# Weight pools laid at whole pages from the stationary tiles, and the down products split in halves around the up group, in a one-core fp32 encoder block

## The chip, the cores and the metric

The kernel runs on one core of one Trainium2 chip. The metric is the device time of one execution in microseconds (us). The kernel before took 1651.87 us, the median of three runs (1650.79, 1651.87 and 1653.72). Its engines are called by their names in the profile: PE is the matrix engine, PEld its loads of stationary tiles, DVE the vector engine, ACT the scalar engine, POOL the GpSimd engine, SP the queue that issues the DMAs.

## The reference

One layer on an input of 256 rows by 2048 columns, all in float32, with a last RMSNorm behind it:

```python
xn = rms_norm(h, norm1_g)
z_a, q, c_kv, q_idx, k_idx, w_idx, gates = split(xn @ w_in)
y_a = spatial_gating_unit(gelu(z_a), ...)          # u * (W_s layer_norm(v) + b)
y_b = indexer_sparse_attention(q, rms_norm(c_kv), q_idx, k_idx, w_idx, w_uk, w_uv)
g_a, g_b = split(sigmoid(gates))
h = h + (g_a * (y_a @ w_oa) + g_b * (y_b @ w_ob)) @ w_out
hn = rms_norm(h, norm2_g)
h = h + (silu(hn @ w_ff_gate) * (hn @ w_ff_up)) @ w_ff_down     # 2048 -> 5632 -> 2048
return rms_norm(h, final_g)
```

## The kernel before

**Three products for one.** Every large product is split into high and low parts. `split` (lines 70 to 78) makes `h` on ACT (line 74) and `l`, the rest, on DVE (line 75). `mm3` (lines 88 to 91) issues three matmuls for each pair of tiles: high by high, high by low, low by high. A matmul keeps a stationary tile of 128 x 128 and streams a moving tile of up to 512 columns past it; while it streams, PE loads the stationary tile of the next one (PEld).

**The first part: everything up to the second norm.** The weights come in chunks of 128 x 1024 through `wchunk` (lines 80 to 86): a DMA into `raw`, ACT makes `wh`, DVE makes `wl`, all three in the pool `wp` with four buffers each. Two helpers consume them. `nat_group` (lines 93 to 106) has the activations stationary and 512 columns of `wh` or `wl` moving; it does the groups named `v`, `u`, `g` (gates), `oa`, `ob`, `out` and `vv`. A group over 16 steps of 128 rows is 16 x 2 x 3 = 96 matmuls; `vv` has 4 steps and 24. There are 4 groups each of `v`, `u`, `oa`, `ob`, `out` and `vv`, and 8 of `g`. `tr_group` (lines 108 to 126) has it the other way round, the weights stationary and 256 columns of the activations moving: 2 groups `qi` and 4 groups `q` of 192 matmuls, and 4 groups `k` of 48.

**Where the tiles lie.** Pools take their places in a partition in the order in which they are opened (lines 48 to 56): `const`, `tp` (20 tiles of 4096 bytes: all activations in high and low parts), then `np` (11 tiles of 4096), `sp` (small tiles of many sizes, 17,376 bytes together), `tq` (4 tiles of 4096) and `wp` (12 tiles of 4096). The build's addresses are 18,336 for `tp`, 100,256 for `np`, 145,312 for `sp`, 162,688 for `tq` and 179,072 for `wp`. A page here means 4096 bytes. `sp` is four pages and 992 bytes long, so `tq` and `wp` begin 992 bytes past a whole number of pages from `tp`. From each other `tq` and `wp` are whole pages. The attention output `yb` of its first two groups is kept in `tq`, that of the last two in `tp`; so the first 48 matmuls of an `ob` group have stationary tiles whole pages from the moving ones, and the last 48 do not.

**The second part: the feed-forward.** `pre.close()` (line 497) gives back `np`, `sp`, `tq` and `wp`, and the pools `wq` and `fp` take their room directly behind `tp` and whole pages from it. `wq` has three buffers for `raw` tiles of 128 x 2048, three each for `wh` and `wl` of that size, two each of 128 x 1536, and one for `sums`. The gate and up products go through `s_group` (lines 520 to 572), a Strassen form that needs seven products for eight. It takes eight weight quads in the order `(0, 4, 1, 5, 2, 3, 6, 7)`. For a quad below 4, DVE first makes four sums of the raw weights (lines 534 to 536), then both the raw quad (1536 columns) and the sums (2048) are split, and PE runs 21 matmuls, of which the first nine need the raw quad alone (from the second such quad on). For the others only the raw quad is split, and PE runs 24. A group is 4 x 21 + 4 x 24 = 180 matmuls of 512 columns. `plain_group` (lines 574 to 585) is the plain form.

The loop at the end runs over five pairs of blocks, counted from 0. One turn is: the gate group `fg` of pair i, with the 16 transposes `a_pt` of the block before (through `beside`, line 558) ahead of its last 12 matmuls; the down products `fd` of pair i-1, which are four groups n of 8 x 2 x 3 = 48 matmuls; the up group `fu` of pair i. PE's order is the order of the program; DVE, ACT and SP get theirs from the scheduler, each a fixed list that is worked off in order. After an up group DVE has to combine its sums (lines 569 and 571) and to multiply by the gate (line 608); after each down group it adds the result to `hn[n]` (line 617).

Of the kernel before, what the change touches and what calls it, by code (L numbers as in the profile page):

```python
# [13 lines left out]
ALU = mybir.AluOpType  # L14
AX = mybir.AxisListType

P = 128
# [23 lines left out]
def block_kernel(ctx: ExitStack, tc: tile.TileContext, a, out):  # L41
# [5 lines left out]
    nc = tc.nc  # L47
# [3 lines left out]
    aux_p = ctx.enter_context(tc.tile_pool(name="aux", bufs=4, space=bass.MemoryType.PSUM))  # L51
    pre = ExitStack()
    np_ = pre.enter_context(tc.tile_pool(name="np", bufs=11))
    sp = pre.enter_context(tc.tile_pool(name="sp", bufs=1))
    tq = pre.enter_context(tc.tile_pool(name="tq", bufs=4))
    wp = pre.enter_context(tc.tile_pool(name="wp", bufs=4))

    def t_tile(name, dt=F32R):
        return tp.tile([P, 4, T], dt, tag="T", name=name)
# [10 lines left out]
    def split(h, l, src, scale=None):  # L70

        hf = h.bitcast(F32)
        if scale is None:
            nc.scalar.activation(h, src, AF.Copy)  # L74
            nc.vector.tensor_tensor(l, src, hf, op=ALU.subtract)  # L75
        else:
            nc.scalar.activation(h, src, AF.Copy, scale=scale)
            nc.vector.scalar_tensor_tensor(l, src, scale, hf, op0=ALU.mult, op1=ALU.subtract)
# [9 lines left out]
    def mm3(o, lh, ll, rh, rl, start, stop, **kw):  # L88
        nc.tensor.matmul(o, lh, rh, start=start, stop=False, **kw)  # L89
        nc.tensor.matmul(o, lh, rl, start=False, stop=False, **kw)  # L90
        nc.tensor.matmul(o, ll, rh, start=False, stop=stop, **kw)  # L91

    def nat_group(w, ks, x, name):


        acc = [acc_tile(f"{name}_{t}") for t in range(2)]
        for c in range(len(ks) // 2):
            wh, wl = wchunk(w[c], 1024)
            for j in range(2):
                i = 2 * c + j  # L100
                xh, xl = x(ks[i])
                for t in range(2):
                    s = slice(t * P, (t + 1) * P)
                    mm3(acc[t], xh[:, s], xl[:, s], wh[:, j * 512:(j + 1) * 512],
                        wl[:, j * 512:(j + 1) * 512], i == 0, i == len(ks) - 1)
        return acc
# [109 lines left out]
    def row_rstd(ss, name):  # L216
        s2 = sp.tile([P, 2], F32, name=f"{name}_s2")
        nc.vector.tensor_reduce(s2, ss.rearrange("p n t -> p t n"), axis=AX.X, op=ALU.add)
        r = const.tile([P, 2], F32, name=f"{name}_r")
        rsqrt(r, s2, 1.0 / D, EPS, 2, name)  # L220
        return r
# [92 lines left out]
    for t in (1, 0):  # L314
        w = (t + 1) * P
        nc.vector.memset(score[t][0:CHUNK, w - CHUNK:w], NEG)
        for i in range(TOPK // 8):
# [4 lines left out]
                                op0=ALU.is_gt, op1=ALU.mult)  # L322
# [104 lines left out]
    for n in range(4):  # L427
        for j in range(2):
# [5 lines left out]
                                           op0=ALU.add, op1=ALU.mult)  # L434
# [4 lines left out]
    def of(pairs):  # L439
        def f(k):  # L440
            h, l = pairs[k // 4]
            return h[:, k % 4], l[:, k % 4]
        return f
# [10 lines left out]
    for n in range(4):  # L454
        ga = gate(n)
        acc = nat_group(a["w_oa"][n], KS, of(ya), f"oa{n}")
# [3 lines left out]
    for n in range(4):  # L460
        gb = gate(4 + n)
        acc = nat_group(a["w_ob"][n], KS, of(yb), f"ob{n}")
# [9 lines left out]
    hn, hT = [], []  # L472
    for n in range(4):
        hx = tp.tile([P, 2, 512], F32, tag="T", name=f"h{n}")
        nc.sync.dma_start(hx, x_nat[n])
        acc = nat_group(a["w_out"][n], KS, of(mx_t), f"out{n}")
# [6 lines left out]
        else:  # L483
            for b in range(2):
                k = 4 * n + 2 * b
# [8 lines left out]
    r2 = row_rstd(ss2, "r2")  # L494
# [6 lines left out]
    def f_tile(name):  # L501
        return fp.tile([P, 2, 512], F32, tag="F", name=name, bufs=3)

    def quad(src):
        raw = wq.tile([P, 4, 512], F32, tag="raw", name="raw")
        nc.sync.dma_start(raw, src)
        return raw

    def quad_split(raw, n=4):
        h, l = (wq.tile([P, n, 512], F32R, tag=f"w{z}{n}", name=f"w{z}", bufs=n - 1 if n < 4 else 3) for z in "hl")  # L510
        split(h, l, raw)
        return h, l
# [61 lines left out]
    def plain_group(chunks, x, n_k, name, bank=acc_tile):  # L574

        acc = [bank(f"{name}_{t}") for t in range(2)]
        for i, c in enumerate(chunks):
            wh, wl = quad_split(quad(c))
            for j in range(4):
                k = 4 * i + j  # L580
                for t in range(2):
                    xh, xl = x(k, t)
                    mm3(acc[t], xh, xl, wh[:, j], wl[:, j], k == 0, k == n_k - 1)
        return acc

    at = {}

    def a_operand(b, s):
        h, l = t_tile(f"ah{b}"), t_tile(f"al{b}")
        transposed(s, f"a{b}", h, l)  # L590
        at[b] = (h, l)

    def gate_blocks(i, beside):
        f, _ = s_group(a["w_fg"][i], f"fg{i}", beside)
        s = [f_tile(f"s{i}_{j}") for j in range(2)]
        for j in range(2):
            for t in range(2):
                f(t, j, s[j][:, t])
                nc.scalar.activation(s[j][:, t], s[j][:, t], AF.Silu, scale=r2[:, t:t + 1])
        return s  # L600

    def up_blocks(i, s):
        f, u = s_group(a["w_fu"][i], f"fu{i}")
        for j in range(2):
            for t in range(2):
                f(t, j)
        for j in range(2):
            nc.vector.tensor_tensor(s[j], s[j], u[:, 2 * j:2 * j + 2], op=ALU.mult)

    def down(b0, n_b):  # L610

        for n in range(4):
            acc = plain_group([a["w_fd"][n, b0 + j] for j in range(n_b)],
                              lambda k, t: tuple(z[:, k % 4, t * P:(t + 1) * P] for z in at[b0 + k // 4]),
                              4 * n_b, f"fd{n}", aux_tile if n < 2 else acc_tile)
            for t in range(2):
                nc.vector.scalar_tensor_tensor(hn[n][:, t], acc[t], r2[:, t:t + 1], hn[n][:, t],
                                               op0=ALU.mult, op1=ALU.add)
            yield n

    def plain_x(k, t):
        if k < 2 * NS:
# [6 lines left out]
    b = NFB - 1  # L629
    for i in range(b // 2 + 1):  # L630
        done = s

        def transposes():
            if done is not None:
                for j in range(2):
                    a_operand(2 * i - 2 + j, done[j])
        if i < b // 2:
            s = gate_blocks(i, transposes)
            if i:
                for _ in down(2 * i - 2, 2):  # L640
                    pass
            up_blocks(i, s)

    acc = plain_group([a["w_fg10"][c] for c in range(4)], plain_x, KT, f"fg{b}", aux_tile)
    transposes()
# [3 lines left out]
    acc = plain_group([a["w_fu10"][c] for c in range(4)], plain_x, KT, f"fu{b}")  # L649
    for t in range(2):  # L650
        nc.vector.tensor_tensor(s[:, t], acc[t], s[:, t], op=ALU.mult)
    kept = []
    for n in down(b - 2, 2):
        if n < 2:
            raw = quad(a["w_fd"][n, b])
            kept.append([])
            for c in range(2):
                h, l = (tp.tile([P, 2, 512], F32R, tag="T", name=z) for z in ("kept_h", "kept_l"))
                split(h, l, raw[:, 2 * c:2 * c + 2])
                kept[n] += [(h[:, k], l[:, k]) for k in range(2)]  # L660
        if n == 1:
            a_operand(b, s)
# [6 lines left out]
    for i in range(2):  # L669
        f = f_tile(f"fg{i}")  # L670
# [106 lines left out]
```

## Time and profile before

| what | us |
|---|---|
| median of three runs | 1651.87 |
| the profiled execution | 1649.41 |
| its span | 1647.6 |
| PE busy | 1608.0 |
| DVE busy | 1098.7 |
| ACT busy | 778.8 |

In the profile a matmul's record is longer than the time to the next one's start, since matmuls are pipelined; the pace of PE is read from the starts. A timeline gives the start of each instruction, its length, the engine, the line, the operation, the tile written and the tiles read, the shapes, and in square brackets the idle time of the engine ahead of it with what ended it. The first feed-forward matmul starts at 898.23 us.

### The profile page before, as it was taken

To read this page: it belongs to the slowest core of one execution; us is meant where nothing else is said; L and a number is where in the kernel's file an instruction comes from. 1 tells how busy PE (TensorE), PEld (TensorE's weight loads), DVE (VectorE), ACT (ScalarE), POOL (GpSimd) and SP (SyncE) were. 2 spreads that over 40 slices of the span, in tenths; PEclk is the share of its full clock that TensorE was granted. 3 is DMA by queue.
4 is the path that set the end of the run, shared out by engine and by line. 5 is a ranking of instruction groups with operands and counts; after the bars stand their busy time and mean duration, and the time that the engine had idled before them with its cause. 6 is when DMAs were issued, how large, how long until landed. Compare 5 with 4: busy or idle time off the path is not lost.

```text
span 1647.6 us, 19647 instructions
## 1 busy us (share of the span) xinstructions
PE 1608.0 (98%) x7834; PEld 1337.3 (81%) x7834; DVE 1098.7 (67%) x1208; ACT 778.8 (47%) x815; POOL 1.6 (0%) x8
## 2 busy tenths in 40 slices
PE   9999999999999999999997998999999999999997
PEld 8988989989788888888885777887887788788886
DVE  5795665565744444555565888788788778777565
ACT  6654454554544444444354464454454544454442
POOL 0000000000000000000000000000000000000000
PEclk9999999999999999999998999999999999999999
DMA  8645545545455555555664544554564554555561
GB/s 304 224 138 191 186 163 182 180 163 192 137 180 191 187 185 190 188 183 183 200 205 157 188 181 176 205 200 163 200 222 161 204 204 179 182 201 198 210 230 51
DMA packets 69115, 307.48 MB, mean 187 GB/s; under 512 B 8160, under 2 KB 8416, under 8 KB 52128
## 3 DMA queue, kind: packets, MB, share of 16 engines
q1 hardware_dynamic: 69024, 306.24, 53.4%
q8 instruction: 61, 1.00, 0.2%
q14 instruction: 30, 0.25, 0.0%
HBM read 304.11 MB, written 2.10 MB: 186 GB/s over the span
## 4 chain that ended last, share of the span: by engine, by line
PE 77%; DVE 12%; ACT 4%; issue 4%; DMA 2%; ACTq 0%; SPq 0%; DVEq 0%
DVE wl L75 7%; ACT wh L74 4%; PE fd L91 4%; PE fd L90 4%; PE fd L89 4%; PE g L89 4%; PE g L90 4%; PE g L91 4%; PE u L91 2%; PE q L123 2%; PE oa L90 2%; PE oa L89 2%; PE v L90 2%; PE v L89 2%; PE u L89 2%
## 5 line engine op out<-in xcount | busy, mean ns | idle before, releaser
L75 DVE TENSOR_TENSOR wl<-raw,wh 128x1024 fp32r<-128x1024 f32 (+3 forms) x434 | 640.3, 1477 | 406.9 <-ACT wh L74 406.6
L74 ACT ACTIVATE wh<-raw 128x1024 fp32r<-128x1024 f32 (+3 forms) x434 | 545.2, 1262 | 578.8 <-PE g L91 90.0
L74 ACT ACTIVATE wh<-sums 128x2048 fp32r<-128x2048 f32 x40 | 76.7, 1917 | 173.8 <-DVE sums L536 152.6
L75 DVE TENSOR_TENSOR wl<-sums,wh 128x2048 fp32r<-128x2048 f32 x40 | 91.7, 2292 | 64.3 <-ACT wh L74 64.3
L89 PE MATMUL fd<-wh,ah 128*128 128x512 f32 x320 | 124.6, 389 | 0.0
L91 PE MATMUL fd<-wh,al 128*128 128x512 f32 x320 | 124.5, 389 | 0.0
L90 PE MATMUL fd<-wl,ah 128*128 128x512 f32 x320 | 124.5, 389 | 0.0
L91 PE MATMUL g<-wh,xl 128*128 128x512 f32 x256 | 102.5, 400 | 0.0
L89 PE MATMUL g<-wh,xh 128*128 128x512 f32 x256 | 102.3, 400 | 0.0
L90 PE MATMUL g<-wl,xh 128*128 128x512 f32 x256 | 101.5, 396 | 0.0
L121 PE MATMUL q<-xh,wh 128*128 128x256 f32 x256 | 71.5, 279 | 0.0
L123 PE MATMUL q<-xl,wh 128*128 128x256 f32 x256 | 71.5, 279 | 0.0
L124 PE MATMUL q<-xh,wl 128*128 128x256 f32 x256 | 71.5, 279 | 0.0
L90 PEld LDWEIGHTS fd<-wl,ah 128*128 128x128 f32 x320 | 60.1, 188 | 12.5
L89 PEld LDWEIGHTS fd<-wh,ah 128*128 128x128 f32 x320 | 60.1, 188 | 12.5
L91 PEld LDWEIGHTS fd<-wh,al 128*128 128x128 f32 x320 | 60.1, 188 | 12.4
L90 PE MATMUL fg_c<-wl,hh 128*128 128x512 f32 x160 | 62.6, 392 | 0.5 <-DVE wl L75 0.5
L89 PE MATMUL fg_c<-wh,hh 128*128 128x512 f32 x160 | 63.0, 393 | 0.0
L91 PE MATMUL fg_c<-wh,hl 128*128 128x512 f32 x160 | 62.4, 390 | 0.0
L89 PE MATMUL fu_c<-wh,hh 128*128 128x512 f32 x160 | 62.2, 389 | 0.0
L90 PE MATMUL fu_c<-wl,hh 128*128 128x512 f32 x160 | 62.2, 389 | 0.0
L91 PE MATMUL fu_c<-wh,hl 128*128 128x512 f32 x160 | 62.2, 389 | 0.0
(303 smaller groups left out, 3431.6 us busy)
## 6 DMA issues: line engine op xcount, KB each, us to landing
raw<-in_w_fg SPq DMA_DIRECT2D x44, 1024.0 KB, 4.8
raw<-in_w_fu SPq DMA_DIRECT2D x44, 1024.0 KB, 4.8
raw<-in_w_fd SPq DMA_DIRECT2D x44, 1024.0 KB, 4.8
raw<-in_w_z SPq DMA_DIRECT2D x64, 512.0 KB, 3.5
raw<-in_w_g SPq DMA_DIRECT2D x64, 512.0 KB, 3.3
raw<-in_w_q SPq DMA_DIRECT2D x32, 512.0 KB, 3.2
raw<-in_w_oa SPq DMA_DIRECT2D x32, 512.0 KB, 3.2
raw<-in_w_ob SPq DMA_DIRECT2D x32, 512.0 KB, 3.2
```

Of the source, the lines that this page charges most:

```text
L74: nc.scalar.activation(h, src, AF.Copy)
L75: nc.vector.tensor_tensor(l, src, hf, op=ALU.subtract)
L89: nc.tensor.matmul(o, lh, rh, start=start, stop=False, **kw)
L90: nc.tensor.matmul(o, lh, rl, start=False, stop=False, **kw)
L91: nc.tensor.matmul(o, ll, rh, start=False, stop=stop, **kw)
L121: nc.tensor.matmul(o, wh[:, s], xh, start=(i == 0 and ct % 2 == 0), stop=False, skip_group_check=True)
L123: nc.tensor.matmul(o, wh[:, s], xl, start=False, stop=False, skip_group_check=True)
L124: nc.tensor.matmul(o, wl[:, s], xh, start=False, stop=last, skip_group_check=True)
```

## The change

The pool `sp` is opened last, behind `wp`. In the build `tq` then begins at 145,312, `wp` at 161,696 and `sp` at 210,848: `wp` is now 35 pages from `tp`. The generator `down` over all four n becomes `down_one` for one n, the turn calls it for n = 0 and 1 behind the gate group and for n = 2 and 3 behind the up group, and the accumulators of the down products alternate between the two PSUM pools (before: n = 0 and 1 in one, 2 and 3 in the other).

```diff
     np_ = pre.enter_context(tc.tile_pool(name="np", bufs=11))
-    sp = pre.enter_context(tc.tile_pool(name="sp", bufs=1))
     tq = pre.enter_context(tc.tile_pool(name="tq", bufs=4))
     wp = pre.enter_context(tc.tile_pool(name="wp", bufs=4))
+    sp = pre.enter_context(tc.tile_pool(name="sp", bufs=1))
...
-    def down(b0, n_b):
-        for n in range(4):
-            acc = plain_group([a["w_fd"][n, b0 + j] for j in range(n_b)],
...
-                              4 * n_b, f"fd{n}", aux_tile if n < 2 else acc_tile)
...
-            yield n
+    def down_one(b, n):
+        acc = plain_group([a["w_fd"][n, b + j] for j in range(2)],
...
+                          8, f"fd{n}", acc_tile if n % 2 else aux_tile)
...
             s = gate_blocks(i, transposes)
-            if i:
-                for _ in down(2 * i - 2, 2):
-                    pass
+            for n in (0, 1) if i else ():
+                down_one(2 * i - 2, n)
             up_blocks(i, s)
+            for n in (2, 3) if i else ():
+                down_one(2 * i - 2, n)
...
-    for n in down(b - 2, 2):
+    for n in range(4):
+        down_one(b - 2, n)
```

On PE, at the end of up group 1, gate group 2 (`fg_m`) followed at once:

```order
L89 MATMUL fu_c_8714<-wh,hh_7517 128x512
L90 MATMUL fu_c_8714<-wl,hh_7517 128x512
L91 MATMUL fu_c_8714<-wh,hl_7518 128x512
L89 MATMUL fg_m_8987<-wh,hS_h 128x512
L90 MATMUL fg_m_8987<-wl,hS_h 128x512
L91 MATMUL fg_m_8987<-wh,hS_l 128x512
```

and in the changed kernel a down group does:

```order
L89 MATMUL fu_c_8586<-wh,hh_7517 128x512
L90 MATMUL fu_c_8586<-wl,hh_7517 128x512
L91 MATMUL fu_c_8586<-wh,hl_7518 128x512
L89 MATMUL fd_0_8859<-wh,ah_8397 128x512
L90 MATMUL fd_0_8859<-wl,ah_8397 128x512
L91 MATMUL fd_0_8859<-wh,al_8398 128x512
```

So 96 matmuls of the down products now stand between an up group and the next gate group, and 96 instead of 192 between a gate group and its up group (from turn 1 on; turn 0 has none).

On DVE, at the same place, the list before went from combining the up group (`fu_c`, then `s`, the product with the gate) straight to the sums of the second quad of the next gate group and their split:

```order
L571 TENSOR_TENSOR fu_u<-fu_c_8714,fu_u 128x512
L608 TENSOR_TENSOR s_0_8441<-s_0_8441,fu_u 128x1024
L608 TENSOR_TENSOR s_1_8442<-s_1_8442,fu_u 128x1024
L534 TENSOR_TENSOR sums<-raw 128x1024
L535 TENSOR_TENSOR sums<-sums,raw 128x512
L75 TENSOR_TENSOR wl<-raw,wh 128x1536
L536 TENSOR_TENSOR sums<-sums,raw 128x512
L75 TENSOR_TENSOR wl<-sums,wh 128x2048
```

In the changed kernel the same sums stand behind the additions of the last down group (`h`, `fd`), with the first quad's sums split, and two further `wl`, ahead of them:

```order
L535 TENSOR_TENSOR sums<-sums,raw 128x512
L536 TENSOR_TENSOR sums<-sums,raw 128x512
L75 TENSOR_TENSOR wl<-sums,wh 128x2048
L75 TENSOR_TENSOR wl<-raw,wh 128x1536
L75 TENSOR_TENSOR wl<-raw,wh 128x2048
L617 SCALAR_TENSOR_TENSOR h_7367<-fd_0_8923,r_r,h_7367 128x512
L617 SCALAR_TENSOR_TENSOR h_7367<-fd_1_8924,r_r,h_7367 128x512
L534 TENSOR_TENSOR sums<-raw 128x1024
L535 TENSOR_TENSOR sums<-sums,raw 128x512
L536 TENSOR_TENSOR sums<-sums,raw 128x512
L75 TENSOR_TENSOR wl<-sums,wh 128x2048
```

The combining of the up group has moved ahead, to the start of the second half of the down products. On SP the loads follow PE's order (the first place where they differ):

```order
 L506 DMA raw<-in_w_fg 128x2048 x8
-L506 DMA raw<-in_w_fd 128x2048 x8
+L506 DMA raw<-in_w_fd 128x2048 x4
 L506 DMA raw<-in_w_fu 128x2048 x8
+L506 DMA raw<-in_w_fd 128x2048 x4
 L506 DMA raw<-in_w_fg 128x2048 x8
```

The down products' eight loads are split into four ahead of the up group's and four behind them.

## Rows read from the trace of the kernel before

**Rows 1.** The page, its head: span, busy time and share, instructions of each engine.

```profile
span 1647.6 us, 19647 instructions
PE 1608.0 (98%) x7834; PEld 1337.3 (81%) x7834; DVE 1098.7 (67%) x1208; ACT 778.8 (47%) x815; POOL 1.6 (0%) x8
```

**Rows 2.** Windows: length, busy us by engine (count), granted clock, DMA share, GB/s.

```profile
429.70:893.00 463.30, 463.30 (x2025) 372.27 (x2023) 238.40 (x235) 199.58 (x222) 0.00 (x0) 1.00 0.55 186
1041.00:1174.00 133.00, 130.00 (x574) 106.80 (x573) 107.54 (x87) 62.63 (x42) 0.00 (x0) 0.99 0.53 192
```

**Rows 3.** Timeline of PE: first matmul of one oa group, and of the g group behind.

```profile
462.67 0.40 PE L89 MATMUL oa<-wh,yah 128*128 128x512 f32 x1
...
485.07 0.40 PE L89 MATMUL g<-wh,xh 128*128 128x512 f32 x1
```

**Rows 4.** Timeline of PE in one ob group: 44 intervals in each half.

```profile
642.56 0.39 PE L89 MATMUL ob<-wh,ybh 128*128 128x512 f32 x1
...
652.54 0.40 PE L91 MATMUL ob<-wh,ybl 128*128 128x512 f32 x1
...
653.47 0.40 PE L89 MATMUL ob<-wh,ybh 128*128 128x512 f32 x1
...
663.74 0.40 PE L91 MATMUL ob<-wh,ybl 128*128 128x512 f32 x1
```

**Rows 5.** Timeline of PE: first matmul of up group 1, and of gate group 2.

```profile
1089.04 0.39 PE L89 MATMUL fu_m<-wh,hS_h 128*128 128x512 f32 x1
...
1129.84 0.39 PE L89 MATMUL fg_m<-wh,hS_h 128*128 128x512 f32 x1
```

**Rows 6.** Timeline of PE, 256 columns: 192 intervals of q, 23 of last.

```profile
176.78 0.28 PE L121 MATMUL q<-xh,wh 128*128 128x256 f32 x1
...
199.19 0.28 PE L121 MATMUL k<-cT_h,wh 128*128 128x256 f32 x1
...
1624.82 0.28 PE L89 MATMUL last<-wh,ah 128*128 128x256 f32 x1
...
1627.57 0.28 PE L91 MATMUL last<-wh,al 128*128 128x256 f32 x1
```

**Rows 7.** Chain of work that ended last: start, us, what; the transposes of four turns.

```profile
1041.17 1.75 PE a_pt L152 x16
...
1173.62 1.75 PE a_pt L152 x16
...
1305.05 1.75 PE a_pt L152 x16
...
1438.22 1.75 PE a_pt L152 x16
```

**Rows 8.** Timeline of PE in gate group 2: its 55th and 56th matmul.

```profile
1142.59 0.51 PE L89 MATMUL fg_m<-wh,hS_h 128*128 128x512 f32 x1 [0.34 <-ACT wh L74]
1144.92 0.50 PE L90 MATMUL fg_m<-wl,hS_h 128*128 128x512 f32 x1 [1.82 <-DVE wl L75]
```

**Rows 9.** Timeline of DVE at the start of gate group 2.

```profile
1131.65 1.28 DVE L569 TENSOR_TENSOR fu_u<-fu_c,fu_u 128x512 f32<-128x512 f32 x2
...
1134.05 2.35 DVE L608 TENSOR_TENSOR s<-s,fu_u 128x1024 f32<-128x1024 f32 x2
1136.31 1.22 DVE L534 TENSOR_TENSOR sums<-raw 128x1024 f32<-128x1024 f32 x1
...
1138.18 1.75 DVE L75 TENSOR_TENSOR wl<-raw,wh 128x1536 fp32r<-128x1536 f32 x1
...
1142.57 2.29 DVE L75 TENSOR_TENSOR wl<-sums,wh 128x2048 fp32r<-128x2048 f32 x1 [2.04 <-ACT wh L74]
```

**Rows 10.** Timeline of ACT in the down groups that start at 1045.5 us.

```profile
1056.64 1.92 ACT L74 ACTIVATE wh<-raw 128x2048 fp32r<-128x2048 f32 x1 [3.52 <-PE fd L91]
```

**Rows 11.** Timeline of DVE where those down groups end and up group 1 starts.

```profile
1088.90 1.40 DVE L617 SCALAR_TENSOR_TENSOR h<-fd,r_r,h 128x512 f32<-128x512 f32 x2
1091.23 2.29 DVE L75 TENSOR_TENSOR wl<-sums,wh 128x2048 fp32r<-128x2048 f32 x1 [0.93 <-ACT wh L74]
```

More of the change, by code (lines that the diff above doesn't have):

```diff
@@ L608, in up_blocks @@
             nc.vector.tensor_tensor(s[j], s[j], u[:, 2 * j:2 * j + 2], op=ALU.mult)
-    def down(b0, n_b):
-        for n in range(4):
-            acc = plain_group([a["w_fd"][n, b0 + j] for j in range(n_b)],
-                              lambda k, t: tuple(z[:, k % 4, t * P:(t + 1) * P] for z in at[b0 + k // 4]),
-                              4 * n_b, f"fd{n}", aux_tile if n < 2 else acc_tile)
-            for t in range(2):
-                nc.vector.scalar_tensor_tensor(hn[n][:, t], acc[t], r2[:, t:t + 1], hn[n][:, t],
-                                               op0=ALU.mult, op1=ALU.add)
-            yield n
+    def down_one(b, n):
+        acc = plain_group([a["w_fd"][n, b + j] for j in range(2)],
+                          lambda k, t: tuple(z[:, k % 4, t * P:(t + 1) * P] for z in at[b + k // 4]),
+                          8, f"fd{n}", acc_tile if n % 2 else aux_tile)
+        for t in range(2):
+            nc.vector.scalar_tensor_tensor(hn[n][:, t], acc[t], r2[:, t:t + 1], hn[n][:, t],
+                                           op0=ALU.mult, op1=ALU.add)
     def plain_x(k, t):
```

## The prediction

> **What bounds the kernel now.** I read the page's head first: PE is busy for 1608.0 of 1647.6 us [rows 1], so time can come only from PE's pace or from its waits. The windows tell which of the two it is in each part [rows 2]. From 429.7 to 893 us PE is busy for all of 463.30 us at a granted clock of 1.00, with DVE at 238.40 and ACT at 199.58 us; there only the pace counts. From 1041 to 1174 us, one turn of the feed-forward, PE is idle for 3.0 of 133 us and DVE is busy for 107.54; there are waits as well. So I read the pace from the starts of matmuls, then the length of the turns, then the lists of DVE and ACT around a wait.
>
> The pace. 96 matmuls of an oa group take 485.07 - 462.67 = 22.40 us, 233.3 ns each [rows 3]. 180 matmuls of an up group take 1129.84 - 1089.04 = 40.80 us, 226.7 ns each [rows 5]. Both are 128x512 in fp32r, at the full clock. What differs is where the tiles lie: in the feed-forward moving and stationary tiles are whole pages (or half pages, the slices being 2048 bytes) apart, in the first part 992 bytes off. The ob group tells the two apart within 22 us: 44 intervals of its first half, with stationary tiles in tq, take 9.98 us, 226.8 ns each, and 44 of its second half, stationary in tp, 10.27 us, 233.4 ns each [rows 4]. Engines, weights and shape are the same in both halves. Hence the place of the tiles sets 6.6 ns of each 512-column matmul.
>
> The waits. The same transposes come at 1041.17, 1173.62, 1305.05 and 1438.22 us [rows 7], so three turns take 132.45, 131.43 and 133.17 us. PE's work in a turn is 192 + 180 + 180 = 552 matmuls at 226.7 ns and the transposes' 1.75 us [rows 5, 7], 126.9 us. The turns lose 5.6, 4.5 and 6.3 us, 16.4 together. The up group loses nothing: its 40.80 us are the pace itself [rows 5]. All is lost in the gate group that follows it. There the 55th and 56th matmul, the first that need the sums of the second quad, start 12.8 and 15.1 us behind the group's start [rows 8], where the pace would have them at 12.2 and 12.5. DVE is late because its list first combines the finished up group, from 1131.65 to 1136.31 us, and only then makes those sums and their split, done at 1144.86 us [rows 9].
>
> **The change, part by part.** *The pools.* Nothing is added or removed in the first part; each matmul there gets another distance between its two tiles. Of 512 columns and now off the page: v, u, oa, out 4 x 96 each, g 8 x 96, the second halves of four ob groups 4 x 48, vv 4 x 24; that is 2592. I take 226.7 for 233.3 ns: 2592 x 6.6 = 17.1 us less. All of it lies on the path, since PE never idles there [rows 2] and DVE and ACT are busy for about half of the stretch; 3% more pace leaves them far behind.
>
> [...]
>
> The transposed groups have 256 columns: q 4 x 192, qi 2 x 192, k 4 x 48, 1344 matmuls, now at 22.41 / 192 = 116.7 ns [rows 6]. No row shows one of these on whole pages. The bounds: half of 226.7, 113.3 ns, would gain 4.6 us; the 256-column matmuls of the last stage, whose tiles are whole pages apart, run at 2.75 / 23 = 119.6 ns [rows 6] and would cost 1344 x 2.9 = 3.9 us. I take the second, a row of the same shape and type. It also fits the numbers: off the page 233.3 is twice 116.7, so the cost goes with the columns; on the page 226.7 less 119.6 is 107.1 ns for 256 columns, which leaves some 12.5 ns per matmul whatever its length. That makes whole pages better for 512 columns and worse for 256.
>
> [...]
>
> The kv groups at the start read other slices (296 columns), with the DMAs at their densest; I cost them at nothing, and if PE alone set them, 192 matmuls times up to 6.6 ns would be 1.3 us either way. sp keeps its distance to tp within a page (it moved by sixteen whole pages), so scores and attention stay as they are. The feed-forward's tiles do not move. At its start they fall on other old tiles than before, wp's for the last wl buffers; those are free with the last out matmul, before the first gate group's splits are reached, so I count nothing.
>
> *The halves.* Turns 1 to 4 now go gate, 96 down matmuls, up, 96 down matmuls. Matmuls, splits, DMAs and additions are the same in number; SP's list is split the same way, and each load still has two tiles of lead, so I count nothing for it. What moves is when DVE can catch up. A half takes PE 96 x 226.7 = 21.8 us and asks of DVE four splits of at most 2.29 and two pairs of additions of 1.40 [rows 11], 12.0 us; 9.8 us are over. In the down groups now, ACT waits 3.52 us for PE to give back a buffer 11 us after the start [rows 10], so the lead is full within half a set already. Behind the second half DVE has only the additions left, which end 1.3 us into the next group [rows 11]. In the changed list the sums of the second quad come next; in rows 9 their chain runs from 1136.31 to 1144.86 us, 8.5 us, with a split of the raw quad of 1.7 us in it that the new list has already done. So it ends 1.3 + 6.8 = 8.1 us into the gate group, where 12.5 are allowed; now it ends at 15.0. The combining of the up group, 4.7 us in rows 9, lies in the half of down products, where 9.8 us are free. Carried on with the same durations, the pair of sum quads in the middle of the group (2 and 3 of the order) comes out even: ready within 0.2 us of its due time. I leave 0.2 us for each of the three gate groups. The up groups start behind half a down set in place of a whole one, with the same full lead and the same order of additions and splits; I cost them at nothing, and the price if they are not covered is the third rival. Gate groups 0 and 1 and up group 0 have no down products ahead of them and keep their losses. So 16.4 - 0.6 = 15.8 us go.
>
> **The sum.** 17.1 - 3.9 + 15.8 = 29.0 us. The profiled execution took 1649.4 us, so it would be 1620.4; the median of the runs is 2.5 us above the profile's execution, 1651.9 - 29.0 = 1622.9. I say 1622, between the two.
>
> **The rivals.** *The 256-column matmuls gain too*, to 113.3 ns: 8.5 us less than forecast, 1614; unchanged they would give 1618. For it: nothing but symmetry; against it: the rows of the last stage. Chance 0.15.
>
> *Half of the gate groups' loss stays.* The sum quads in the middle of the group have no slack in my reckoning, and the granted clock of a turn is 0.99, not 1.00 [rows 2], so a wait may cost more than its length: 8 us more, 1630. Chance 0.08.
>
> *Half a down set is too short.* DVE has to win back the 6.9 us by which it is late in rows 9 (15.0 in place of 8.1); it has 9.8 us free. If it wins back less, every group, up groups as well, starts as late as the gate groups do now, since the additions of line 617 also hold the accumulators that the next group needs. Seven groups (up 1 to 4, gate 2 to 4) at 5.5 us are 38, against 16.4 now: 22 us more, less the 13.2 of the pools, 1651.9 + 8.8 = 1661, slower than before. It decides where DVE's free time in a half falls under 6.9 us; rows 10 speak against it. Chance 0.03.
>
> *The layout does nothing*: the two halves of ob would then differ for another reason, such as the pool tq itself. Only the halves of down count, 1651.9 - 15.8 = 1636. Chance 0.05. [...] Neither part working, 1652, gets 0.01.
>
> **How the numbers follow.** The forecast has 0.68, with 4 us on either side for the middle sums, kv and the spread of the runs. The range takes in the first rival at its lower end, 1612, and the second at its upper, 1632; outside are the third, the fourth and part of the edges, some 0.12. A measurement of this kernel can tell about 0.2%, 3.3 us, from no change. Faster: the forecast and the rivals but the third, 0.96; the same 0.01; slower 0.03.
>
> **What would show it.** In the changed profile an oa group takes 21.76 us in place of 22.40, and both halves of an ob group have one pace; a set of 192 q matmuls takes 22.96 in place of 22.41 us, or 21.76 by the first rival. The first feed-forward matmul comes 13 us sooner. The transposes of the turns stand 126.9 to 127.2 us apart, and from gate group 2 on PE waits for no wl of DVE by more than 0.5 us. The forecast is wrong if the 512-column pace stays at 233, if q goes below 116, or if a gate or up group from turn 1's up group on loses over 1 us.

## The result, and the profile after

The changed kernel takes 1626.6 us, the median of four runs (1625.2 to 1628.29), and the kernel before, in the same session, 1651.82. The ratio is 0.9846, with an interval of 0.9829 to 0.9864: faster by 25.2 us where the sum had 29.0, and inside the range of 1612 to 1632. The profiled execution took 1625.63 us; its page begins so, beside [rows 1]:

```profile
span 1623.8 us, 19653 instructions
PE 1593.5 (98%) x7834; PEld 1340.2 (83%) x7834; DVE 1098.9 (68%) x1208; ACT 777.9 (48%) x815; POOL 1.6 (0%) x8
```

The span lost 23.8 us, of which PE's busy time lost 14.5; the work of DVE and ACT is what it was. The windows of the changed kernel that answer to [rows 2], with the same columns, the first from the first g group to where the tail of the last out group is under way, the second one turn:

```profile
430.14:882.66 452.52, 452.52 (x2025) 371.55 (x2023) 238.44 (x235) 199.67 (x222) 0.00 (x0) 1.00 0.58 191
1032.00:1159.40 127.40, 127.15 (x569) 105.26 (x568) 106.90 (x87) 62.31 (x42) 0.00 (x0) 1.00 0.55 197
```

The same 2025 matmuls take 452.52 in place of 463.30 us at the same granted clock of 1.00: that is pace. In a turn PE is idle for 0.25 us where it was idle for 3.0: those are waits.

The pace, in the timeline of PE in the changed kernel, the rows that answer to [rows 6], [rows 3] and [rows 4]:

```profile
175.51 0.28 PE L121 MATMUL q<-xh,wh 128*128 128x256 f32 x1
...
198.54 0.28 PE L121 MATMUL k<-cT_h,wh 128*128 128x256 f32 x1
...
462.62 0.39 PE L89 MATMUL oa<-wh,yah 128*128 128x512 f32 x1
...
484.38 0.39 PE L89 MATMUL g<-wh,xh 128*128 128x512 f32 x1
...
636.70 0.39 PE L89 MATMUL ob<-wh,ybh 128*128 128x512 f32 x1
...
646.68 0.39 PE L91 MATMUL ob<-wh,ybl 128*128 128x512 f32 x1
...
647.58 0.39 PE L89 MATMUL ob<-wh,ybh 128*128 128x512 f32 x1
...
657.56 0.39 PE L91 MATMUL ob<-wh,ybl 128*128 128x512 f32 x1
```

The oa group takes 21.76 us, 226.7 ns a matmul, as forecast. The two halves of the ob group, 44 intervals each, both take 9.98 us. The 192 matmuls of q take 23.03 us, 120.0 ns each, where 22.96 were forecast: 256 columns became slower, as the sum had it.

The turns, in the chain of work that ended last (start, us, what), beside [rows 7]:

```profile
1032.17 1.75 PE a_pt L152 x16
...
1159.60 1.75 PE a_pt L152 x16
...
1287.06 1.75 PE a_pt L152 x16
...
1414.53 1.75 PE a_pt L152 x16
```

They stand 127.43, 127.46 and 127.47 us apart, 382.4 together in place of 397.1. In gate group 2, PE's timeline has its first matmul and the only one that waited:

```profile
1120.81 0.39 PE L89 MATMUL fg_m<-wh,hS_h 128*128 128x512 f32 x1
...
1148.64 0.50 PE L90 MATMUL fg_m<-wl,hS_h 128*128 128x512 f32 x1 [0.25 <-DVE wl L75]
```

and DVE's timeline at the start of that group, beside [rows 9], has the splits of the second and of the fourth quad's sums (one of four such quads in a group):

```profile
1126.76 2.29 DVE L75 TENSOR_TENSOR wl<-sums,wh 128x2048 fp32r<-128x2048 f32 x1 [2.06 <-ACT wh L74]
...
1146.30 2.29 DVE L75 TENSOR_TENSOR wl<-sums,wh 128x2048 fp32r<-128x2048 f32 x1 [2.07 <-ACT wh L74]
```

The second quad's sums are split at 1129.05, 8.2 us into the group (forecast: 8.1, before: 15.0). The fourth quad's are split at 1148.59; they are due with the group's 122nd matmul, which the pace would have had at 1148.24, so PE comes 0.4 us late. It is the only wait of the group.

### The profile page after: what moved, and what is told of

It is laid out like the page before. It is cut to its first block, busy times and chain, and to the rows that moved or that the text cites. A ratio compares the mean times of both kernels' runs of the same rounds, so it can differ in the third digit from the quotient of the medians.

```text
span 1623.8 us, 19653 instructions
## 1 busy us (share of the span) xinstructions
PE 1593.5 (98%) x7834; PEld 1340.2 (83%) x7834; DVE 1098.9 (68%) x1208; ACT 777.9 (48%) x815; POOL 1.6 (0%) x8
## 4 chain that ended last, share of the span: by engine, by line
PE 88%; DVE 7%; ACT 2%; issue 1%; DMA 0%; ACTq 0%; SPq 0%; DVEq 0%
PE fd L91 4%; PE fd L90 4%; PE fd L89 4%; DVE wl L75 4%; PE g L91 4%; PE g L90 4%; PE g L89 4%; PE fu_c L91 2%; PE fu_c L90 2%; PE fu_c L89 2%; ACT wh L74 2%; PE q L121 2%; PE q L124 2%; PE q L123 2%; PE u L91 2%; PE u L89 2%
## 5 line engine op out<-in xcount | busy, mean ns | idle before, releaser
L90 PEld LDWEIGHTS fd<-wl,ah 128*128 128x128 f32 x320 | 60.1, 188 | 12.5
```

## The experiments

**Each part alone.** Two kernels undo one part each. The first keeps the new order of the pools and takes back the split of the down products:

```diff
-            for n in (0, 1) if i else ():
-                down_one(2 * i - 2, n)
+            if i:
+                for _ in down(2 * i - 2, 2):
+                    pass
             up_blocks(i, s)
-            for n in (2, 3) if i else ():
-                down_one(2 * i - 2, n)
```

> Only the pool sp is moved behind wp; the down products stay whole behind the gate group. If the distance of the tiles sets PE's pace: oa groups of 21.76 us, q sets of 23.0 us, first feed-forward matmul at 888 us, turns of 132 us as before; 1651.8 - 10.3 = 1641.5 us. If instead the first part gained through something else (the split of the down products changed the scheduler's order there too), oa stays at 22.40 us and the time at 1652.

It took 1641.85 us (1640.42 to 1645.04), a ratio of 0.9942, interval 0.993 to 0.9955. PE's timeline has the new pace in the oa group (21.76 us) and the first feed-forward matmul at 888.38:

```profile
463.06 0.39 PE L89 MATMUL oa<-wh,yah 128*128 128x512 f32 x1
...
484.82 0.39 PE L89 MATMUL g<-wh,xh 128*128 128x512 f32 x1
...
888.38 0.77 PE L89 MATMUL fg_m<-wh,hS_h 128*128 128x512 f32 x1 [3.27 <-ACT wh L74]
```

and its chain has the old turns, 131.37 us in this one as 131.43 in [rows 7]:

```profile
1165.00 1.75 PE a_pt L152 x16
...
1296.37 1.75 PE a_pt L152 x16
```

The second keeps the split and puts `sp` back in its old place:

```diff
+    sp = pre.enter_context(tc.tile_pool(name="sp", bufs=1))
     tq = pre.enter_context(tc.tile_pool(name="tq", bufs=4))
     wp = pre.enter_context(tc.tile_pool(name="wp", bufs=4))
-    sp = pre.enter_context(tc.tile_pool(name="sp", bufs=1))
```

> Only the down products are split in halves; sp stays ahead of tq and wp. If the two parts are independent: oa groups of 22.40 us, first feed-forward matmul at 898 us, turns of 127.4 us as in the changed kernel; 1651.8 - 14 = 1638 us (13 if gate group 1 loses the 1.5 us more that it lost there, 14.6 if not). If the halves needed the new layout, turns stay over 130 us and the time over 1645.

It took 1637.14 us (1634.9 to 1637.86), 0.991, interval 0.9897 to 0.9924. Its oa group takes 22.40 us, its first feed-forward matmul comes at 898.39, and its chain has the new turn, 127.43 us:

```profile
1168.91 1.75 PE a_pt L152 x16
...
1296.34 1.75 PE a_pt L152 x16
```

So the pools alone give 9.6 us and the halves alone 14.3, each against the 1651.43 us of that session; 23.9 together, and the change as a whole gave 25.2. Within the spread of the runs the two parts add up, so neither needs the other. With this the rival that the layout does nothing has fallen. The alternating accumulators of the down products came with the halves and were not run apart from them; in the kernel before, the down groups (192 matmuls in 43.52 us) and the up groups (180 in 40.80) ran at PE's pace throughout, so they had no wait there that other accumulators could have removed.

**How short may a part be?** The rival on the slow side had a threshold. Two kernels split the down products one to three and three to one:

```diff
-            for n in (0, 1) if i else ():
+            for n in (0,) if i else ():
...
-            for n in (2, 3) if i else ():
+            for n in (1, 2, 3) if i else ():
```

> The changed kernel with one of four down groups behind the gate group and three behind the up group. A quarter takes PE 10.9 us and asks 6.0 of DVE, so 4.9 us are free, less than the 6.9 by which DVE is late. If that is what decides: each of the four up groups of turns 1 to 4 loses 1 to 4 us, gate groups 2 to 4 lose 0.4 us as now; 1626.6 + 4 to 16 = 1631 to 1643 us. If a quarter is enough: within 1 us of 1626.6.

It took 1629.28 us (1628.64 to 1629.95), 0.9865, interval 0.9851 to 0.9878. The forecast was too pessimistic. One wait stands out, in the first up group, in PE's timeline (42.94 us for the group's 40.80):

```profile
1048.17 0.39 PE L89 MATMUL fu_m<-wh,hS_h 128*128 128x512 f32 x1
...
1077.60 0.50 PE L90 MATMUL fu_m<-wl,hS_h 128*128 128x512 f32 x1 [1.82 <-DVE wl L75]
...
1091.11 0.39 PE L89 MATMUL fd<-wh,ah 128*128 128x512 f32 x1
```

The later up groups lose 0.5, 0.5 and 0.8 us, the gate groups behind the three others nothing.

The other way round:

```diff
-            for n in (0, 1) if i else ():
+            for n in (0, 1, 2) if i else ():
...
-            for n in (2, 3) if i else ():
+            for n in (3,) if i else ():
```

> The changed kernel with three of four down groups behind the gate group and one behind the up group: the short cover is now ahead of gate groups 2 to 4. If a quarter is too short: these three lose 2 to 5 us each in place of 0.6, 1626.6 + 4 to 13 = 1631 to 1640 us, up groups lose nothing. If a quarter is enough: within 1 us of 1626.6.

It took 1629.33 us (1627.53 to 1629.67), 0.9866, interval 0.9851 to 0.9881. The gate groups 2 to 4 lose 1.3, 1.2 and 1.3 us, again at the fourth quad's sums, as PE's timeline of gate group 2 shows:

```profile
1148.34 0.50 PE L90 MATMUL fg_m<-wl,hS_h 128*128 128x512 f32 x1 [1.03 <-DVE wl L75]
```

The expectation that the up groups lose nothing did not hold: those of turns 1 to 3 lose 0.2, 0.5 and 0.2 us, and the single down group behind each 0.1.

One down group is 48 x 226.7 ns = 10.9 us long and covers nearly all that four covered. A whole set behind one group and none behind the other was the bad arrangement; how the set is divided matters little, and the even division was the best of the three: by 2.7 us between medians, which the intervals alone do not prove, but the groups' losses point the same way (1.7 us in the turns of the even division, 3.9 and 5.1 in those of the others).

**Which distance?** That it is the distance, and not the place of one of the two tiles, follows for 512 columns from the addresses: modulo 256 bytes (what is left over whole multiples of 256), `tq` and `wp` began at 128 and `tp` at 160 in the kernel before, and all three begin at 160 now. Moving tiles at 128 ran at both paces (the two halves of ob, 226.8 and 233.4 ns), and so did stationary tiles at 160 (the second half of ob, 233.4 ns before and 226.8 now). Whole pages cannot be the rule itself: within one group the tiles' slices move by 512 bytes from step to step, and the pace is even (PE's timeline has 2.80 us for every 12 matmuls of the oa group of [rows 3], and 2.71 to 2.73 in the changed kernel). The next kernel makes the weight tiles 1152 columns wide and gives each g, oa and q group its own start within them (with three buffers for `raw`, for room; its start is some 10 us longer, its one run took 1639.26 us, and it is read for the pace alone):

```diff
-        raw = wp.tile([P, 1024], F32, tag="raw", name="raw")
-        h = wp.tile([P, 1024], F32R, tag="wh", name="wh")
-        l = wp.tile([P, 1024], F32R, tag="wl", name="wl")
+        raw = wp.tile([P, 1024], F32, tag="raw", name="raw", bufs=3)
+        h = wp.tile([P, 1152], F32R, tag="wh", name="wh")[:, off:off + 1024]
+        l = wp.tile([P, 1152], F32R, tag="wl", name="wl")[:, off:off + 1024]
...
+        acc = tr_group(a["w_q"][n], KS, x_of, f"q{n}", off=(0, 8, 16, 4)[n])
+        acc = nat_group(a["w_g"][g], KS, x_of, f"g{g}", (0, 8, 16, 4, 64, 24, 32, 120)[g])
+        acc = nat_group(a["w_oa"][n], KS, of(ya), f"oa{n}", (0, 8, 12, 40)[n])
```

> The changed kernel with wh and wl tiles of 1152 columns (their starts are 512 bytes, not whole pages, apart) and three raw buffers; each group's weights start at its own offset in the tile: the eight g groups at 0, 32, 64, 16, 256, 96, 128 and 480 bytes, oa at 0, 32, 48 and 160, q at 0, 32, 64 and 16. If whole pages are what counts: only the tile that lies at whole pages and offset 0 runs at 226.7 ns, a quarter of g0 and oa0, all else at 233.3. If only the distance modulo 64 bytes counts: g at 0, 64, 256 and 128 run at 226.7 ns (21.76 us a group), g at 32, 96 and 480 at 233.3 (22.40 us); oa at 0 fast, at 32 and 160 slow; 16 and 48 bytes open. q (192 matmuls): 23.04 us at 0 and 64 bytes, 22.41 at 32.

PE's timeline has the oa group at 0 bytes (21.76 us), a g group at 32 (22.40) and one at 256 (21.76); and of the q groups the one at 64 bytes (335.05 less 313.28 = 21.77 us):

```profile
313.28 0.28 PE L121 MATMUL q<-xh,wh 128*128 128x256 f32 x1
...
335.05 0.28 PE L121 MATMUL k<-cT_h,wh 128*128 128x256 f32 x1
...
471.52 0.39 PE L89 MATMUL oa<-wh,yah 128*128 128x512 f32 x1
...
493.28 0.40 PE L89 MATMUL g<-wh,xh 128*128 128x512 f32 x1
...
515.68 0.39 PE L89 MATMUL oa<-wh,yah 128*128 128x512 f32 x1
...
626.88 0.39 PE L89 MATMUL g<-wh,xh 128*128 128x512 f32 x1
...
648.64 0.39 PE L89 MATMUL ob<-wh,ybh 128*128 128x512 f32 x1
```

The groups that run through, read in the same way from the starts, with the kernel before for 224 bytes (992 less three times 256):

| bytes off | 512 columns, 96 matmuls, us | ns each | 256 columns, 192 matmuls, us | ns each |
|---|---|---|---|---|
| 0 | 21.76 | 226.7 | 23.03 | 120.0 |
| 16 | 22.24 | 231.7 | 22.72 | 118.3 |
| 32 | 22.40 | 233.3 | 22.72 | 118.3 |
| 48 | 22.08 | 230.0 | | |
| 64 | 21.99 | 229.0 | 21.77 | 113.4 |
| 160 | 22.49 | 234.3 | | |
| 224 (before) | 22.40 | 233.3 | 22.41 | 116.7 |
| 256 | 21.76 | 226.7 | | |

The g groups at 96, 128 and 480 bytes are broken up by the transposes mx_pt. In the chain the four sets of those stand 45.09, 44.99 and 45.01 us apart, with a g and an ob group of 96 between two of them, where the changed kernel has 44.48, 44.47 and 44.48; ob is at 0 bytes in both, so these three are slow as well, by 5 to 6 ns a matmul. Both theories of the expectation have fallen: 256 bytes are as fast as 0, and 64 are not. At 512 columns 0 and 256 bytes are fast; `sp` at its old place left the tiles 992 bytes off, 32 short of four times 256, with 233.3 ns; 32 bytes to the other side give the same here. At 256 columns 0 is the worst distance tried, and 64 bytes give the 113.4 ns of the first rival: the change gave the long matmuls their distance and took it from the short ones. The two sides are not alike there: 118.3 ns at 32 bytes, 116.7 at 224. For 256 columns the runs moved the weights alone, so the place of the weights by itself is not excluded.

**A version with both distances.** High and low half in one tile with 256 bytes to spare, so that four buffers for `raw` still fit; the groups of 256 columns start 64 bytes in, all others at 0:

```diff
-    def wchunk(src, cols):
+    def wchunk(src, cols, off=0):
         raw = wp.tile([P, 1024], F32, tag="raw", name="raw")
-        h = wp.tile([P, 1024], F32R, tag="wh", name="wh")
-        l = wp.tile([P, 1024], F32R, tag="wl", name="wl")
+        hl = wp.tile([P, 2112], F32R, tag="whl", name="whl")
+        h = hl[:, off:off + 1024]
+        l = hl[:, off + 1024:off + 2048]
...
-    def tr_group(w, ks, x, name, bank=acc_tile, beside=None):
+    def tr_group(w, ks, x, name, bank=acc_tile, beside=None, off=16):
...
-            wh, wl = wchunk(w[c], 1024)
+            wh, wl = wchunk(w[c], 1024, off)
```

> The changed kernel with one thing more: of each weight chunk, the high and the low half lie in one tile with 256 bytes to spare (four such tiles, 1,024 bytes more in all), so that a group can choose where in it they stand. The groups whose moving tile has 256 columns (q, qi and k) put them 64 bytes further, all others leave them where the change has them. Theory that the distance of the two tiles by itself sets the pace, and that 256 columns want another distance than 512: the q groups' 192 matmuls take 21.77 us as at 64 bytes in the look at offsets (113.4 ns) and not 23.03, the k groups' 48 some 5.44 instead of 5.76, qi the same as q, oa stays at 21.76; 1344 matmuls gain 6.6 ns each = 8.8 us, of which all counts but what a wait hides (the k groups' share, 4 x 0.3 us, may lie behind the softmax chain): 1617.5 to 1619. Theory that the pace at 64 bytes came from the three raw buffers or the start of that look: q stays at 23.03 and the time at 1626.6. Theory that one tile for both halves delays the first matmul of a chunk (it would wait for the low half too): the weight chunks arrive with room to spare in the attention half, so nothing but the first groups (kv) could show it.

It took 1621.66 us (1619.33 to 1622.41), 0.9808, interval 0.9794 to 0.9821, clear of the change's 0.9829 to 0.9864: it beats both kernels. But it gained some 5 us and not 8, and PE's timeline shows why, in the first and the last q group with the k group behind each:

```profile
175.41 0.28 PE L122 MATMUL q<-xh,whl 128*128 128x256 f32 x1
...
198.02 0.28 PE L122 MATMUL k<-cT_h,whl 128*128 128x256 f32 x1
...
364.83 0.28 PE L122 MATMUL q<-xh,whl 128*128 128x256 f32 x1
...
386.61 0.28 PE L122 MATMUL k<-cT_h,whl 128*128 128x256 f32 x1
```

The last q takes 21.78 us, 113.4 ns each, the first 22.61, 117.8 ns, at the same distance. The second and the third q take 22.61 us as well; of the two qi groups one takes 21.78 and one 22.70; the k behind each q has the pace of its q (5.65 us, 117.7 ns each, behind the first and 5.44, 113.3 ns, behind the last). There are two paces at one distance, and no q took a time between the two. No q takes 23.03 us any more, so the pace at 64 bytes did not come from the three raw buffers. The kv groups end 1.3 us later in this profile (the first qi starts at 33.59 in place of 32.27), which would fit the third theory; but with the same tiles the profile of the last kernel below has it at 32.25.

In the same session q ran at four more distances:

```diff
-        acc = tr_group(a["w_q"][n], KS, x_of, f"q{n}")
+        acc = tr_group(a["w_q"][n], KS, x_of, f"q{n}", off=(24, 32, 48, 64)[n])
```

> As the one before, but the four q groups put their weights 96, 128, 192 and 256 bytes further (qi and k stay at 64). With the look before (0: 23.03 us for 192 matmuls, 16 and 32: 22.72, 64: 21.77) this shows the pace at 256 columns over a whole turn. If 256 columns follow the same period as 512: 256 bytes gives 23.03 again. If a distance to either side counts alike: 192 bytes gives 21.77. If every offset but a whole 256 is better: 96, 128 and 192 all lie below 22.8.

They took 22.53 us at 96 bytes, 22.78 at 128, 21.76 at 192 and 23.03 at 256, the last of these in PE's timeline:

```profile
362.68 0.28 PE L122 MATMUL q<-xh,whl 128*128 128x256 f32 x1
...
385.71 0.28 PE L122 MATMUL k<-cT_h,whl 128*128 128x256 f32 x1
```

So 256 bytes give at 256 columns what 0 gives, as they do at 512, and 192, which is 64 to the other side, gave what 64 gives. The k groups are all at 64 bytes here; from the first matmul of k to the next q it is 40.30 us behind the q at 192 bytes and 40.53 behind those at 96 and 128. The time was 1621.74 us, one run. Last, all groups of 256 columns at 192 bytes:

```diff
-    def tr_group(w, ks, x, name, bank=acc_tile, beside=None, off=16):
+    def tr_group(w, ks, x, name, bank=acc_tile, beside=None, off=48):
```

> All groups of 256 columns put their weights 192 bytes further, where the version before had 64. There the q groups showed two paces at one and the same distance: 22.61 us for 192 matmuls in three of them (117.8 ns) and 21.77 in the fourth (113.4), and k after each q kept its pace; at 192 bytes the one q group looked at took 21.76. Theory that 192 bytes always gives 113.4 ns: every q and qi at 21.77, k at 5.44; against the version before 3 x 0.84 + 3 x 0.21 + 0.93 = 4.1 us less, 1617.5. Theory that at both distances the pace hangs on how the group's first matmul fell in time: some groups at 21.77, others near 22.6, and the time between 1617.5 and 1622.5.

It took 1622.89 us (1620.4 to 1624.32), 0.9817, interval 0.9804 to 0.9831. PE's timeline has both paces again, 22.61 us in the first q and 21.76 in the second:

```profile
174.91 0.28 PE L122 MATMUL q<-xh,whl 128*128 128x256 f32 x1
...
197.52 0.28 PE L122 MATMUL k<-cT_h,whl 128*128 128x256 f32 x1
...
238.01 0.28 PE L122 MATMUL q<-xh,whl 128*128 128x256 f32 x1
...
259.77 0.28 PE L122 MATMUL k<-cT_h,whl 128*128 128x256 f32 x1
```

The third q was fast (21.76 us) and the fourth slow (22.62). From the first matmul of k to the next q it is 40.32 and 40.30 us behind the two fast q and 40.49 behind the first. That fits a k that takes the pace of the q ahead of it, whatever the distance of that q. Which of the two paces a group takes is not settled by its distance; that it hangs on the instant of its first matmul fits all of this, but no run varied that by itself, and it stays open.

## Why the prediction was right, and where it was off

The likeliest case came true: PE's pace at 512 columns rose with the layout, it fell at 256, and the gate groups' waits went with the halves. Its sum was too large, by 3.8 us between the medians (25.2 in place of 29.0) and by 5.2 between the profiled executions (23.8). Where the 5.2 are:

| stretch | forecast, us | measured, us |
|---|---|---|
| up to the first feed-forward matmul (898.23, now 887.89) | -13.2 | -10.3 |
| from there to the a_pt of turn 1 (142.9, now 144.3) | 0 | +1.3 |
| the three turns (397.1, now 382.4) | -15.8 | -14.7 |
| the rest (209.4, now 209.3) | 0 | -0.1 |

**The pace of 512 columns: right in size, its place on the path not everywhere.** 6.6 ns a matmul are shown (233.3 to 226.7 in oa, g and ob, and by the pools alone, which gave 9.6 us). The step that failed is "All of it lies on the path, since PE never idles there": [rows 2] show it from 429.7 us on, behind the attention turns. In the four attention turns a group of 96 u matmuls lies between the links of the softmax chain, and there the chain sets the time. In the kernel before, PE's timeline has the last att matmul and the transpose pT of one softmax, with the last u matmul ahead of it:

```profile
219.92 0.38 PE L387 MATMUL att<-k,q 128*128 128x128 f32 x2
...
224.10 0.40 PE L90 MATMUL u<-wl,xh 128*128 128x512 f32 x1
224.45 0.30 PE L403 MATMUL pT<-ident,z 128*128 128x128 f32 x1
```

and the timeline of all engines of the changed kernel has the same links with those between them:

```profile
219.16 0.38 PE L387 MATMUL att<-k,q 128*128 128x128 f32 x2
...
219.58 0.56 DVE L391 TENSOR_TENSOR z<-att,keep 128x384 f32<-128x384 f32 x1 [1.12 <-PE att L387]
...
222.99 0.55 DVE L401 TENSOR_SCALAR z<-z,sm 128x256 f32<-128x256 f32 x2
...
223.68 0.30 PE L403 MATMUL pT<-ident,z 128*128 128x128 f32 x1
```

4.53 us before and 4.52 after, though the u matmuls in between now go 3% faster. From the first att matmul to the next q the time fell from 29.62 to 29.40 us, 0.22 in place of 96 x 6.6 = 0.63; four times that is 1.6 us of the 2.9 missing here. PE was busy for the whole stretch in the kernel before (35.22 of 35.22 us from 204.78 to 240.00), so the busy share could not show it. The starts did: pT comes 0.35 us behind the last u matmul, where one u follows the other by 0.23, and the u record of 0.40 us covers that wait. The chain already set the time there, with no slack for a faster PE to use.

**The pace of 256 columns: right in sign, a little small.** q and qi lose 0.62 us a group, k 0.16: 4.4 us in place of 3.9, 0.5 of the missing. The row taken for it, the last stage's 119.6 ns, was the right one; the reason given, a cost of 12.5 ns a matmul whatever its length, does not carry over to other distances: at 64 bytes 256 columns take 113.4 ns and 512 take 229.0, which leaves nothing of the kind. The first rival was wrong for this change, but right that 113.3 ns can be had. The lowest pace in any of these groups is 113.3 ns, k in 5.44 us. Of the last 0.8 us, 0.6 lie behind the first g group: from there to the first feed-forward matmul 10.8 us went (468.53, now 457.75) where 1728 x 6.6 = 11.4 were counted (g, oa, out and the second halves of ob). Two thirds of these 0.6 are in the stretch of the out groups, among whose matmuls transposes stand; the cause stays open.

**The turns: right.** The gate groups lose 0.55, 0.59 and 0.59 us where 0.2 each were left, for the reason given (the sum quads in the middle of the group come out nearly even; 0.4 us of it is the wait at 1148.64). The up groups lose nothing. The turns were to stand 126.9 to 127.2 us apart and stand 127.4 to 127.5 apart. Half of the gate groups' loss did not stay.

**The start of the feed-forward: costed at nothing, +1.3 us.** Gate group 1 lost 7.65 us, 6.2 in the kernel before. Behind its last wait its matmuls run at half pace for a while, in PE's timeline of the changed kernel:

```profile
1019.61 0.50 PE L90 MATMUL fg_m<-wl,hS_h 128*128 128x512 f32 x1 [1.82 <-DVE wl L75]
...
1020.32 0.63 PE L89 MATMUL fg_m<-wh,hS_h 128*128 128x512 f32 x1
1020.75 0.63 PE L90 MATMUL fg_m<-wl,hS_h 128*128 128x512 f32 x1
```

That is 430 ns from start to start. The window of that stretch (columns as above) has a granted clock of 0.50:

```profile
1020.30:1022.90 2.60, 2.60 (x8) 2.00 (x7) 1.54 (x1) 1.01 (x1) 0.00 (x0) 0.50 0.16 22
```

Seven such intervals cost 7 x 0.2 = 1.4 us. The kernel with three down groups behind the gate group has the same wait of 1.82 us at this place and 0.23 us from start to start behind it, and its gate group 1 lost 6.31 us. The same 0.23 us follow the wait in the kernel before (1.82 us, then a granted clock of 1.00) and in the two versions with all groups of 256 columns at 64 and at 192 bytes (1.83 and 1.82 us). In the chains the a_pt of turn 1 come 12.6 us behind the end of the split that this wait is for in the changed kernel, with the pools alone and with a start for each group, and 11.0 us behind it in the kernel before and with the halves alone. So of these eight kernels three lose time behind the wait and five do not: it does not come with the change as such, and what decides it stays open. In the kernel before, the waits of gate groups 2 and 4 brought such a stretch each (a granted clock of 0.50 from 1146.3 and from 1426.2 us), and that of gate group 3 none (1.00); with the waits they have gone.

**The rival on the slow side** had its threshold too high. It said that DVE needs 6.9 us of free time in each part. With a single down group, 10.9 us of PE's time, DVE has far less (half of the 9.8 counted for a half), and the kernel was still 22 us faster than before, with losses of 0.5 to 2.1 us in a group. The step that failed is that DVE has to win back its whole lateness within one part; where it wins back the rest stays open.

## What to carry to other kernels

When the same matmul runs at two paces at one granted clock (here 233.3 and 226.7 ns at 1.00), compare where its moving and its stationary tile lie, modulo 256 bytes; a pool of odd length opened ahead of the weights cost 3% of PE's pace here, and the best of the distances tried for 512 columns (0 and 256 bytes) was the worst for 256 columns (120.0 ns, 113.4 at 64 bytes). Work that is long on PE and short on DVE is worth more divided between the stages in which DVE is late than spent behind one of them (1626.6 us against 1641.85), and a quarter of it may do (1629.28). A gain in PE's pace counts only where no chain over other engines runs beside it (the softmax chain took 4.53 us before and 4.52 after): read the start of the chain's last link less that of its first, not PE's busy share.

## What was not expected of the hardware

- In these kernels the pace went with the distance of the tiles modulo 256 bytes: 226.7 ns for 512 columns at 0 and 256, 229.0 to 234.3 at the other distances tried. For 256 columns it is the other way round: 120.0 ns at 0 and 256, 113.4 at 64 and 192, between 116 and 119 at 16, 32, 96, 128 and 224.
- For 256 columns with all groups at 64 or at 192 bytes the q groups took 21.76 to 21.78 us (113.4 ns) or 22.61 to 22.62 (117.8), and none a time between; with all at 64 bytes the 48 matmuls of k took 5.65 us behind a slow q and 5.44 behind a fast one.
- A wait of the same length, 1.82 us at the same matmul, was followed by a granted clock of 0.50 in the changed kernel and of 1.00 in the kernel before.
